# Attention scores: the low-half products of two maps on 64 rows each, side by side in the array

## The chip, the cores and the metric

The kernel runs on one core of a Trainium2 chip. The metric is the device time of one execution in microseconds (us). Engines are called as the profile calls them: PE (TensorE matmuls), PEld (TensorE weight loads), DVE (VectorE), ACT (ScalarE), POOL (GpSimd), SP (SyncE, which issues the DMAs).

## The reference

A two-layer encoder trunk in float32, sequence 1024, width 1024: a convolution and gating layer, an MLP, a differential attention layer, an MLP, each with a norm whose shift, scale and gate come from a condition vector. The part that matters is the attention, 8 heads of two softmax maps with 64 channels each:

```python
q = q.reshape(B, S, H, 2, d) * (d ** -0.5)      # d = 64, H = 8, S = 1024
k = k.reshape(B, S, H, 2, d)
v = v.reshape(B, S, H, 2 * d)
...
logits = (jnp.einsum('bqhjd,bkhjd->bhjqk', qb, k).astype(f32)
          + bias.astype(f32)[None, :, None])    # qb: 128 queries
p = jax.nn.softmax(logits, axis=-1)
attn = p[:, :, 0] - lam * p[:, :, 1]
return jnp.einsum('bhqk,bkhe->bqhe', attn.astype(v.dtype), v)
```

## The kernel before

PE takes its operands in a rounded type (`F32R`). For precision each operand is split into a high half (rounded) and a low half (the rest), and a product is made of three: high by high, high by low, low by high (`mm3`, lines 130 to 132). Everything is laid out with channels on partitions.

The attention runs head by head. `qkv(hd)` is a generator that projects the keys, queries and values of a head in six units (`UNITS`); it yields after every k-tile so that the products of the next head's projections can stand between those of this head's attention (`fill`, with counts from `QUOTA`). The last head has no next one, and the output projection's first part (`early`) fills in its place.

A map has 64 channels, half of the 128 rows of the array. The keys of map j are kept in one tile `K[j]` of 128 rows: for map 0 the high halves in rows 0 to 63 and the low halves in rows 64 to 127, for map 1 the other way round. The queries of a unit (512 queries) are kept in four tiles `Q`: high and low halves of map 0, high and low halves of map 1, each written to its own 64 rows by ACT (high) or DVE (low) and copied by a DMA to the other 64 rows. So one product of 128 rows by `Q[2j]` gives high by (high + low), and one by `Q[2j + 1]` gives low by (high + low).

`Head.softmax(qb)` makes the scores of 128 queries against 1024 keys for both maps. A map's scores `S` fill two banks of PSUM (`bufs=2`, so two maps' scores are alive at a time); each of its two halves of 512 keys is one product by the high queries (line 961) and one by the low ones (line 962). Then DVE adds the bias and takes the minimum (line 965), ACT the exponential (line 967), DVE combines both maps (line 975). `turn` transposes the result on PE (line 987) and splits it (ACT line 259, DVE line 260), and `values` multiplies it with the values for two query blocks at once (lines 998 to 1000).

The order on each engine is set by the framework's scheduler from the order in which the code is written, the dependencies, and priorities; engines then run their own lists in order and wait for each other on semaphores. There are 64 softmax blocks: 8 heads of 8 query blocks.

One product elsewhere is smaller than the array: the bias table (line 449), 32 rows and 8 columns, four products of two passes each, at 83 us.

Of the kernel before, what the change touches and what calls it, by code (L numbers as in the profile page):

```python
# [10 lines left out]
F32 = mybir.dt.float32  # L11
F32R = mybir.dt.float32r
AF = mybir.ActivationFunctionType
ALU = mybir.AluOpType
# [4 lines left out]
P = 128  # L19
D = 1024  # L20
T = 1024
KT = D // P
C = 512
NC = T // C
# [23 lines left out]
def trunk(ctx: ExitStack, tc: tile.TileContext, t_in, out):  # L48
    nc = tc.nc
    dve, act, pool, pe, sp = nc.vector, nc.scalar, nc.gpsimd, nc.tensor, nc.sync  # L50

    def f32(ap):
        return ap.bitcast(F32)
# [11 lines left out]
    NOSYNC = mybir.DependencyInfo(mybir.DependencyClass.NoSync, mybir.DependencyReason.DATA)  # L65
# [20 lines left out]
    def load(dst, src):  # L86
        sp.dma_start(out=dst, in_=src)
# [264 lines left out]
    with opened(name="mix", bufs=1) as mp, ExitStack() as pst:  # L352
# [87 lines left out]
        psum = pst.enter_context(opened(name="mixps", bufs=6, space=PSUM))  # L440
# [5 lines left out]
        for j in range(4):  # L446
            js = slice(j * C, (j + 1) * C)
            ps = bank()
# [10 lines left out]
        for j in range(2):  # L459
            dve.tensor_tensor_reduce(out=lv[:, 2 * j, :], in0=lv[:, 2 * j, :], in1=lv[:, 2 * j + 1, :], op0=ALU.mult,  # L460
                                     op1=ALU.add, scale=1.0, scalar=0.0, accum_out=ls[:, j:j + 1])
# [46 lines left out]
        for t in range(8):  # L508
            dve.tensor_scalar(out=vg[t], in0=vg[t], scalar1=mv[:, t, 0:1], scalar2=vr[:, t:t + 1],
                              op0=ALU.subtract, op1=ALU.mult)  # L510


        ps = bank()
        pe.matmul(ps, ones, sgw, start=True, stop=True)
        for g in range(4):
            dve.scalar_tensor_tensor(out=sgb[:, g, :], in0=ps[:, g * P:(g + 1) * P], scalar=vcol(V_SLB + g),
                                     in1=sgb[:, g, :], op0=ALU.mult, op1=ALU.add)
# [372 lines left out]
    if True:  # L890
# [6 lines left out]
        def qkv(hd):  # L897
            K = [ap.tile([P, T], F32R, name=f"K{j}", tag="K", bufs=4) for j in range(2)]
            Vh = ap.tile([P, KT, P], F32R, name="Vh", tag="V", bufs=4)
            Vl = ap.tile([P, KT, P], F32R, name="Vl", tag="V", bufs=4)  # L900
            Q = [None] * NC
            res = (K, Q, Vh, Vl)
            yield res
            for which, c in UNITS[hd > 0]:
                cs = slice(c * C, (c + 1) * C)
                wh, wl = ws.get(3 * hd + which)
                tick()
                ps = bank()
                for k in range(KT):
                    mm3(ps, wh[:, kcol(k)], wl[:, kcol(k)], h[k][c][0], h[k][c][1], k == 0, k == KT - 1)  # L910
                    if k < KT - 1:
                        yield None
                with tc.high_priority(offset=300):
                    if which == 0:
                        act.copy(out=K[0][0:64, cs], in_=ps[0:64])
                        act.copy(out=K[1][64:128, cs], in_=ps[64:128])
                        dve.tensor_tensor(out=K[0][64:128, cs], in0=ps[0:64], in1=f32(K[0][0:64, cs]), op=ALU.subtract)
                        dve.tensor_tensor(out=K[1][0:64, cs], in0=ps[64:128], in1=f32(K[1][64:128, cs]), op=ALU.subtract)
                    elif which == 1:
                        qs = [ap.tile([P, C], F32R, name="Q", tag="Q", bufs=10) for _ in range(4)]  # L920
                        Q[c] = qs
                        act.activation(out=qs[0][0:64], in_=ps[0:64], func=AF.Copy, scale=SC)
                        act.activation(out=qs[2][64:128], in_=ps[64:128], func=AF.Copy, scale=SC)
                        dve.scalar_tensor_tensor(out=qs[1][0:64], in0=ps[0:64], scalar=SC, in1=f32(qs[0][0:64]),
                                                 op0=ALU.mult, op1=ALU.subtract)
                        dve.scalar_tensor_tensor(out=qs[3][64:128], in0=ps[64:128], scalar=SC, in1=f32(qs[2][64:128]),
                                                 op0=ALU.mult, op1=ALU.subtract)
                        for q in (0, 1):
                            load(f32(qs[q][64:128]), f32(qs[q][0:64]))
                            load(f32(qs[2 + q][0:64]), f32(qs[2 + q][64:128]))  # L930
                    else:
                        vT = tmp.tile([P, C], F32, name="vT", tag="ss", bufs=2)
                        act.copy(out=vT, in_=ps)
                        pt = bank()
                        for n in range(4):
                            pe.transpose(pt[:, n * P:(n + 1) * P], vT[:, n * P:(n + 1) * P], ident)
                        vs = slice(c * 4, c * 4 + 4)
                        split(Vh[:, vs, :].rearrange("p a b -> p (a b)"), Vl[:, vs, :].rearrange("p a b -> p (a b)"), pt)
                yield None

        class Head:
# [9 lines left out]
            def softmax(self, qb, fill=None, between=0):  # L951
                c, qs = qb // 4, slice((qb % 4) * P, (qb % 4 + 1) * P)
                win = self.B[:, 896 - P * qb:896 - P * qb + T]
                E, s = [], small.tile([P, 2], F32, name="s", tag="s")
                for j in range(2):
                    if j and fill:
                        fill(between)
                    S = psum.tile([P, T], F32, name="S", tag="S", bufs=2)
                    for n in range(NC):
                        sl = slice(n * C, (n + 1) * C)  # L960
                        pe.matmul(S[:, sl], self.Q[c][2 * j][:, qs], self.K[j][:, sl], start=True, stop=False)
                        pe.matmul(S[:, sl], self.Q[c][2 * j + 1][:, qs], self.K[j][:, sl], start=False, stop=True)
                    L = apr.tile([P, T], F32, name="L", tag="E", bufs=4)
                    mn = small.tile([P, 1], F32, name="mn", tag="mn")
                    dve.tensor_tensor_reduce(out=L, in0=S, in1=win, op0=ALU.add, op1=ALU.min, scale=1.0,  # L965
                                             scalar=3e38, accum_out=mn)
                    act.activation(out=L, in_=L, func=AF.Exp, bias=mn, scale=-1.0, accum_out=s[:, j:j + 1])  # L967
                    E.append(L)

                if qb % 4 == 0:  # L970
                    self.se = small.tile([P, 4], F32, name="se", tag="se", bufs=3)
                r = small.tile([P, 1], F32, name="rs", tag="rs")
                dve.reciprocal(out=r, in_=s[:, 1:2])
                dve.scalar_tensor_tensor(out=r, in0=r, scalar=nlam, in1=s[:, 0:1], op0=ALU.mult, op1=ALU.mult)
                dve.scalar_tensor_tensor(out=E[0], in0=E[1], scalar=r, in1=E[0], op0=ALU.mult, op1=ALU.add)
                dve.scalar_tensor_tensor(out=self.se[:, qb % 4:qb % 4 + 1], in0=s[:, 0:1], scalar=SUB_EPS, in1=s[:, 0:1],
                                         op0=ALU.mult, op1=ALU.mult)
                if qb % 4 == 3:
                    load(sed[self.hd, c].rearrange("n p -> p n"), self.se)
                self.E = E[0]  # L980
# [236 lines left out]
```

## Time and profile before

| | |
|---|---|
| median of 3 runs | 2315.51 us (2313.82 to 2316.77) |
| the profiled execution | 2312.99 us, span 2311.2 us |
| PE busy | 2188.4 us (95%) |
| DVE busy | 1867.0 us (81%) |
| ACT busy | 1180.8 us (51%) |
| POOL busy | 238.5 us (10%) |
| granted TensorE clock, mean | 0.982 |
| scores, lines 961 and 962 | 256 + 256 products, first at 1035.5 us, last at 1583.5 us |

Busy times are those of one profiled execution. Matmuls overlap, and the profile models their ends: a matmul's duration is longer than its slot, the distance from its start to the next one's. PEld lists the loads of the stationary operand; a load that runs beside the matmul before it costs PE nothing.

### The profile page before, as it was taken

The page shows a single profiled execution, that of the slowest core. Times are in us where ns is not written, and L with a number is a line of the kernel's source. Part 1 is how long each engine was busy: PE and PEld are TensorE (multiplying, and loading weights), DVE is VectorE, ACT ScalarE, POOL GpSimd, SP SyncE. Part 2 cuts the span into 40 slices and gives each one's busy share as a digit, 9 for nine tenths or more (in the row PEclk, how much of TensorE's full clock was granted, in tenths as well). Part 3 has the DMA queues.
Part 4 walks back from the last instruction along what each step waited for, and adds up shares of the span by engine and source line. Part 5 has one row for each costly group of instructions (what it writes and reads, how often), then busy time and mean ns, then how long its engine had stood idle before and what let it go on. Part 6 is the DMA issues. An engine that isn't in the chain of part 4 may idle for free. (4 is left out here: it accounts for less than half of the span.)

```text
span 2311.2 us, 27508 instructions
## 1 busy us (share of the span) xinstructions
PE 2188.4 (95%) x10144; PEld 1800.3 (78%) x10144; DVE 1867.0 (81%) x2582; ACT 1180.8 (51%) x1753; POOL 238.5 (10%) x126
## 2 busy tenths in 40 slices
PE   4997599999999999979999999999999999999997
PEld 3786387778888888858888888887778888888886
DVE  8899899997785976986878878876699659578497
ACT  4554246643534535455666666654366354353455
POOL 0484000000000000031111111111100000000002
PEclk9998799999999999989999999999999999999999
DMA  8221553838448267233445333361353461643712
GB/s 319 84 73 46 192 168 131 319 112 284 178 165 284 97 224 250 91 114 90 93 92 109 68 90 73 77 205 51 114 216 121 163 229 48 214 140 111 245 45 73
DMA packets 113863, 335.17 MB, mean 145 GB/s; under 512 B 20576, under 2 KB 23520, under 8 KB 112704
## 3 DMA queue, kind: packets, MB, share of 16 engines
q1 hardware_dynamic: 113728, 333.41, 44.6%
q8 instruction: 80, 1.31, 0.2%
q14 instruction: 55, 0.45, 0.1%
HBM read 279.79 MB, written 53.58 MB: 144 GB/s over the span
## 5 line engine op out<-in xcount | busy, mean ns | idle before, releaser
L131 PE MATMUL ps<-b,whi 128*128 128x512 f32 (+1 forms) x1808 | 701.4, 389 | 6.7 <-DVE b L260 6.7
L130 PE MATMUL ps<-b,whi 128*128 128x512 f32 (+1 forms) x1808 | 692.8, 390 | 5.1 <-ACT b L259 4.6
L132 PE MATMUL ps<-b,wlo 128*128 128x512 f32 (+1 forms) x1808 | 693.6, 388 | 1.9 <-DVE wlo L260 1.9
L259 ACT CAST whi<-raw 128x1024 fp32r<-128x1024 f32 (+1 forms) x225 | 236.5, 1051 | 356.1 <-PE ps L131 310.1
L131 PEld LDWEIGHTS ps<-b,whi 128*128 128x128 f32 x1808 | 340.7, 188 | 79.7 <-DVE b L260 9.5
L130 PEld LDWEIGHTS ps<-b,whi 128*128 128x128 f32 x1808 | 340.3, 188 | 77.0 <-ACT b L259 3.9
L132 PEld LDWEIGHTS ps<-b,wlo 128*128 128x128 f32 x1808 | 340.4, 188 | 72.1 <-DVE wlo L260 2.7
L260 DVE TENSOR_TENSOR wlo<-raw,whi 128x1024 fp32r<-128x1024 f32 x224 | 273.0, 1219 | 137.4 <-ACT whi L259 135.5
L130 PE MATMUL ps<-hh,whi 128*128 128x512 f32 x576 | 225.0, 403 | 40.7 <-ACT hh L254 23.5
L131 PE MATMUL ps<-hl,whi 128*128 128x512 f32 x576 | 229.4, 399 | 4.1 <-DVE hl L255 2.6
L132 PE MATMUL ps<-hh,wlo 128*128 128x512 f32 x576 | 227.9, 396 | 0.0
L113 POOL TENSOR_TENSOR wlo<-raw,whi 128x1024 fp32r<-128x1024 f32 x32 | 83.7, 2619 | 1188.3 <-ACT whi L112 1027.4
L967 ACT ACTIVATE L<-L,mn 128x1024 f32<-128x1024 f32 x128 | 147.1, 1150 | 90.3 <-DVE mn L965 89.0
L748 DVE SCALAR_TENSOR_TENSOR x<-ps,mod,x 128x512 f32<-128x512 f32 x220 | 159.3, 744 | 38.6 <-PE ps L132 38.3
L965 DVE CUSTOM_DVE_ANT_0 L<-S,B 128x1024 f32<-128x1024 f32 x128 | 155.9, 1223 | 37.1 <-PE pt L987 18.2
L130 PEld LDWEIGHTS ps<-hh,whi 128*128 128x128 f32 x576 | 109.7, 191 | 67.9 <-ACT hh L254 27.2
L259 ACT CAST b<-f 128x512 fp32r<-128x512 f32 x192 | 118.0, 618 | 76.5 <-PE ps L132 74.6
L260 DVE TENSOR_TENSOR b<-f,b 128x512 fp32r<-128x512 f32 x192 | 128.6, 683 | 10.0 <-ACT b L259 10.0
L131 PEld LDWEIGHTS ps<-hl,whi 128*128 128x128 f32 x576 | 110.5, 192 | 29.3 <-DVE hl L255 5.5
L132 PEld LDWEIGHTS ps<-hh,wlo 128*128 128x128 f32 x576 | 110.4, 192 | 24.1 <-issue 0.5
L147 DVE CUSTOM_DVE_ANT_0 mraw<-mraw,cact 128x1024 f32<-128x1024 f32 x96 | 116.1, 1217 | 6.2 <-DMA mraw<-in_modw 6.2
L737 ACT COPY f<-ps 128x512 f32<-128x512 f32 x96 | 56.3, 590 | 122.8 <-PE ps L132 122.6
(199 smaller groups left out, 3478.8 us busy)
## 6 DMA issues: line engine op xcount, KB each, us to landing
b<-tspl SPq DMA_DIRECT2D x168, 512.0 KB, 5.2
raw<-in_wm SPq DMA_DIRECT2D x128, 512.0 KB, 4.3
mraw<-in_modw SPq DMA_DIRECT2D x96, 512.0 KB, 4.6
tspl<-b SPq DMA_DIRECT2D x56, 512.0 KB, 4.2
raw<-in_wqkv SPq DMA_DIRECT2D x24, 512.0 KB, 4.7
raw<-in_wo SPq DMA_DIRECT2D x17, 512.0 KB, 3.5
x<-in_xT SPq DMA_DIRECT2D x32, 256.0 KB, 5.8
tsr<-tsp SPq DMA_DIRECT2D x8, 1024.0 KB, 7.7
```

Source lines behind the costliest of these rows:

```text
L113: (eng or dve).tensor_tensor(out=lo, in0=raw, in1=f32(hi), op=ALU.subtract)
L130: pe.matmul(ps, wh, ah, start=first, stop=False, skip_group_check=resumed)
L131: pe.matmul(ps, wh, al, start=False, stop=False, skip_group_check=resumed)
L132: newest[0] = pe.matmul(ps, wl, ah, start=False, stop=last, skip_group_check=resumed)
L147: i = dve.tensor_tensor_reduce(out=raw, in0=raw, in1=cact, op0=ALU.mult, op1=ALU.add, scale=1.0, scalar=0.0, accum_out=acc)
L259: act.copy(out=out_h, in_=src)
L260: (lo_eng or dve).tensor_tensor(out=out_l, in0=src, in1=f32(out_h), op=ALU.subtract)
L737: act.copy(out={"X1": c11, "Y1": c22, "X2": c12}[p], in_=ps)
L748: dve.scalar_tensor_tensor(out=x[m][c], in0=ps, scalar=gate(d, m), in1=x[m][c], op0=ALU.mult, op1=ALU.add)
L965: dve.tensor_tensor_reduce(out=L, in0=S, in1=win, op0=ALU.add, op1=ALU.min, scale=1.0, scalar=3e38, accum_out=mn)
L967: act.activation(out=L, in_=L, func=AF.Exp, bias=mn, scale=-1.0, accum_out=s[:, j:j + 1])
```

## The change

The queries of a unit get three tiles instead of four: the high halves of map 0 and map 1 as before (written to their own 64 rows, copied by DMA to the others), and one tile for the low halves of both maps, map 0 in rows 0 to 63 and map 1 in rows 64 to 127, without a copy. The scores of both maps are allocated before either is reduced. The products by the high halves stay as they are, all 128 rows. The products by the low halves now use only the 64 rows of their own map, in which `K[j]` holds the high keys; the product of low queries with low keys is left out. In the built program these products are laid on the upper half of the array's rows for map 0 and on the lower half for map 1, all 128 columns; for each half of the keys map 0's and map 1's stand one after the other, and an ordering dependency without a semaphore keeps the four behind the last product by the high halves and in their order.

```diff
-                        qs = [ap.tile([P, C], F32R, name="Q", tag="Q", bufs=10) for _ in range(4)]
+                        qs = [ap.tile([P, C], F32R, name="Q", tag="Q", bufs=9) for _ in range(3)]
                         Q[c] = qs
                         act.activation(out=qs[0][0:64], in_=ps[0:64], func=AF.Copy, scale=SC)
-                        act.activation(out=qs[2][64:128], in_=ps[64:128], func=AF.Copy, scale=SC)
-                        dve.scalar_tensor_tensor(out=qs[1][0:64], in0=ps[0:64], scalar=SC, in1=f32(qs[0][0:64]),
-                                                 op0=ALU.mult, op1=ALU.subtract)
-                        dve.scalar_tensor_tensor(out=qs[3][64:128], in0=ps[64:128], scalar=SC, in1=f32(qs[2][64:128]),
-                                                 op0=ALU.mult, op1=ALU.subtract)
-                        for q in (0, 1):
-                            load(f32(qs[q][64:128]), f32(qs[q][0:64]))
-                            load(f32(qs[2 + q][0:64]), f32(qs[2 + q][64:128]))
+                        act.activation(out=qs[1][64:128], in_=ps[64:128], func=AF.Copy, scale=SC)
+                        for j in range(2):
+                            own, other = slice(64 * j, 64 * j + 64), slice(64 - 64 * j, 128 - 64 * j)
+                            dve.scalar_tensor_tensor(out=qs[2][own], in0=ps[own], scalar=SC, in1=f32(qs[j][own]),
+                                                     op0=ALU.mult, op1=ALU.subtract)
+                            load(f32(qs[j][other]), f32(qs[j][own]))
...
+                S = []
                 for j in range(2):
                     if j and fill:
                         fill(between)
-                    S = psum.tile([P, T], F32, name="S", tag="S", bufs=2)
+                    S.append(psum.tile([P, T], F32, name="S", tag="S", bufs=2))
                     for n in range(NC):
                         sl = slice(n * C, (n + 1) * C)
-                        pe.matmul(S[:, sl], self.Q[c][2 * j][:, qs], self.K[j][:, sl], start=True, stop=False)
-                        pe.matmul(S[:, sl], self.Q[c][2 * j + 1][:, qs], self.K[j][:, sl], start=False, stop=True)
+                        before = pe.matmul(S[j][:, sl], self.Q[c][j][:, qs], self.K[j][:, sl], start=True, stop=False)
+                for n in range(NC):
+                    sl = slice(n * C, (n + 1) * C)
+                    for j in range(2):
+                        rows = slice(64 * j, 64 * j + 64)
+                        i = pe.matmul(S[j][:, sl], self.Q[c][2][rows, qs], self.K[j][rows, sl], start=False, stop=True)
+                        tc.add_manual_dep(i.ins, before.ins.name, NOSYNC, reason="side by side")
+                        before = i
+                for j in range(2):
                     L = apr.tile([P, T], F32, name="L", tag="E", bufs=4)
                     mn = small.tile([P, 1], F32, name="mn", tag="mn")
-                    dve.tensor_tensor_reduce(out=L, in0=S, in1=win, op0=ALU.add, op1=ALU.min, scale=1.0,
+                    dve.tensor_tensor_reduce(out=L, in0=S[j], in1=win, op0=ALU.add, op1=ALU.min, scale=1.0,
```

In the lists below `S_` are the scores, `K0` and `K1` the keys of the two maps, `Q_` the query tiles, `pt_` the transposes, `AT_` their split; numbers tell buffers apart. Line numbers of the changed kernel are 4 to 7 higher from the scores on: its line 966 makes the products of 64 rows, 994 the transposes, 1005 and 1006 the products with the values.

PE, the first softmax of a query half in the second head. Before:

```order
L961 MATMUL S_8695<-K0_7812,Q_8284 128x512 [waits DMAHW3_49,DVE_49]
L962 MATMUL S_8695<-K0_7812,Q_8285 128x512 [waits DMAHW6_49]
L961 MATMUL S_8695<-K0_7812,Q_8284 128x512
L962 MATMUL S_8695<-K0_7812,Q_8285 128x512
L961 MATMUL S_8710<-K1_7813,Q_8286 128x512 [waits DMAHW4_49,DVE_49]
L962 MATMUL S_8710<-K1_7813,Q_8287 128x512 [waits DMAHW7_49]
L987 MATMUL pt_8567<-ident_75,L_8441 128x128 [waits DVE_49,PE_49]
L987 MATMUL pt_8567<-ident_75,L_8441 128x128 x7
L961 MATMUL S_8710<-K1_7813,Q_8286 128x512
L962 MATMUL S_8710<-K1_7813,Q_8287 128x512
```

Now:

```order
L961 MATMUL S_8683<-K0_7806,Q_8275 128x512 [waits DMAHW2_49,DVE_49]
L961 MATMUL S_8683<-K0_7806,Q_8275 128x512
L961 MATMUL S_8692<-K1_7807,Q_8276 128x512 [waits DMAHW3_49,DVE_49]
L961 MATMUL S_8692<-K1_7807,Q_8276 128x512
L966 MATMUL S_8683<-K0_7806,Q_8277 128x512
L966 MATMUL S_8692<-K1_7807,Q_8277 128x512
L966 MATMUL S_8683<-K0_7806,Q_8277 128x512
L966 MATMUL S_8692<-K1_7807,Q_8277 128x512
```

The four products by the low halves, which stood behind a product by the high half each, stand together at the end of the block, the two maps in turn; nothing stands between them.

PE, two softmax blocks later in the same head, from the transposes to the first products with the values. Before:

```order
L987 MATMUL pt_8737<-ident_75,L_8587 128x128 x7
L961 MATMUL S_8915<-K0_7812,Q_8284 128x512 [waits DVE_49]
L962 MATMUL S_8915<-K0_7812,Q_8285 128x512
L961 MATMUL S_8915<-K0_7812,Q_8284 128x512
L962 MATMUL S_8915<-K0_7812,Q_8285 128x512
L998 MATMUL ps_8809<-AT_8681,Vh_7814 128x256 [waits Activation_49]
L936 MATMUL ps_8883<-ident_75,vT_8881 128x128 x4
L961 MATMUL S_8930<-K1_7813,Q_8286 128x512 [waits DVE_49]
L962 MATMUL S_8930<-K1_7813,Q_8287 128x512
L961 MATMUL S_8930<-K1_7813,Q_8286 128x512
L962 MATMUL S_8930<-K1_7813,Q_8287 128x512
L999 MATMUL ps_8809<-AT_8682,Vh_7814 128x256 [waits DVE_49]
```

Now:

```order
L994 MATMUL pt_8725<-ident_75,L_8586 128x128 x7
L961 MATMUL S_8749<-K0_7806,Q_8275 128x512 [waits DVE_49]
L961 MATMUL S_8749<-K0_7806,Q_8275 128x512
L131 MATMUL ps_8758<-hl_7401,whi_8612 128x512
L961 MATMUL S_8765<-K1_7807,Q_8276 128x512 [waits DVE_49]
L961 MATMUL S_8765<-K1_7807,Q_8276 128x512
L966 MATMUL S_8749<-K0_7806,Q_8277 128x512
L966 MATMUL S_8765<-K1_7807,Q_8277 128x512
L966 MATMUL S_8749<-K0_7806,Q_8277 128x512
L966 MATMUL S_8765<-K1_7807,Q_8277 128x512
L132 MATMUL ps_8758<-hh_7400,wlo_8613 128x512
L1005 MATMUL ps_8794<-AT_8669,Vh_7808 128x256 [waits Activation_49]
```

Where the first product with the values stood behind four score products and the next behind four more, now a whole block of both maps stands between the transposes and the first of them.

## The prediction

> **What bounds the kernel now.** I read the page first (busy time per engine, granted clock), then the groups by line for the score products, then a table by stretch over the attention stage, then the waits of PE in it, and last the order of time around the one place where this kernel already leaves the full array. First the stage, 1052 to 1583 us, then one whole head:
>
> ```profile
> span 2311.2 us, 27508 instructions
> ...
> 1052.00:1583.00 531.00, 527.08 (x2877) 447.21 (x2876) 431.41 (x708) 323.66 (x508) 82.27 (x39) 1.00 0.42 96
> ...
> 1143.30:1212.50 69.20, 69.02 (x381) 58.78 (x380) 56.23 (x92) 42.73 (x68) 10.72 (x5) 1.00 0.46 91
> ...
> L961 PE MATMUL S<-K,Q 128*128 128x512 f32 x256 | 108.4, 424 | 0.6 <-DVE mn L965 0.6
> ...
> L962 PE MATMUL S<-K,Q 128*128 128x512 f32 x256 | 100.8, 394 | 0.0
> ```
>
> The columns of the table are the stretch, its length, and busy time of PE, PEld, DVE, ACT and POOL, then the granted clock. PE is busy in 527 of 531 us at clock 1.00; DVE, the next, in 56.2 of a head's 69.2 us. So each slot taken from PE here shortens the run, down to DVE's 56 us per head, which is 13 us away. The score products are 512 matmuls in 64 softmax blocks (8 heads, 8 query blocks), 8 in each; half of them (L962) use the low halves.
>
> The mean of 394 or 424 ns is no cost: matmuls overlap. What one costs is the distance between starts:
>
> ```profile
> 1322.86 0.39 PE L132 MATMUL ps<-hh,wlo 128*128 128x512 f32 x1
> ...
> 1325.13 0.39 PE L961 MATMUL S<-K,Q 128*128 128x512 f32 x1
> 1325.35 0.39 PE L962 MATMUL S<-K,Q 128*128 128x512 f32 x1
> ...
> 1324.90 0.19 PEld L961 LDWEIGHTS S<-K,Q 128*128 128x128 f32 x1
> 1325.13 0.19 PEld L962 LDWEIGHTS S<-K,Q 128*128 128x128 f32 x1
> ```
>
> Ten slots from 1322.86 to 1325.13 make 0.227 us each, and each load starts when the matmul ahead of it starts (1325.13 in both lists), so loads are hidden. A softmax block costs 8 x 0.227 = 1.82 us, 116 us in all.
>
> **The change: what it removes.** Four full products by the low halves become four of 64 rows, in two pairs. If a pair took one slot and nothing else changed, a block would lose 2 x 0.227 = 0.454 us, 64 blocks 29.1 us. That is the ceiling, 2283.9 us against the profiled execution's 2312.99.
>
> **What it adds: two changes of the array's shape per block.** All products here use 128 rows, so the trace of before shows no 64-row product. It has one place with a smaller shape, 32 rows and 8 columns (L449, the bias table). Starts around it, PE first, then PEld:
>
> ```profile
> 82.99 0.39 PE L132 MATMUL ps<-hh,wlo 128*128 128x512 f32 x1
> 83.31 1.02 PE L449 MATMUL ps<-oh,tb 32*8 32x512 f32 x2
> ...
> 85.89 1.02 PE L449 MATMUL ps<-oh,tb 32*8 32x512 f32 x2
> 86.84 0.50 PE L130 MATMUL ps<-hh,whi 128*128 128x512 f32 x1
> 87.18 0.39 PE L131 MATMUL ps<-hl,whi 128*128 128x512 f32 x1
> ...
> 82.77 0.19 PEld L132 LDWEIGHTS ps<-hh,wlo 128*128 128x128 f32 x1
> 83.31 0.09 PEld L449 LDWEIGHTS ps<-oh,tb 32*8 32x8 f32 x2 [0.35 <-issue]
> 83.75 0.08 PEld L449 LDWEIGHTS ps<-oh,tb 32*8 32x8 f32 x1 [0.34 <-issue]
> ...
> 86.84 0.19 PEld L130 LDWEIGHTS ps<-hh,whi 128*128 128x128 f32 x1 [0.86 <-issue]
> 86.94 0.19 PEld L131 LDWEIGHTS ps<-hl,whi 128*128 128x128 f32 x1
> ```
>
> Into the small shape: the last full matmul starts at 82.99, its slot ends at 83.22, and the next load starts only at 83.31, though in a full stream it would have started at 82.99. So the load is no longer hidden, and 0.09 us pass first. Out of it: the L449 slots are 0.43 us ((85.89 - 83.31) / 6), the last ends at 85.89 + 2 x 0.43 = 86.75, and the load of L130 starts 0.09 us later, at 86.84, "issue" being time in which it waited for nothing that the profile shows. L131 starts at 87.18, so L130 streamed from 86.95: its exposed load cost 0.11 us. Is the cause the other type (32-bit passes) rather than the shape? At full shape a change of type shows no gap:
>
> ```profile
> 1315.85 0.40 PE L132 MATMUL ps<-hh,wlo 128*128 128x512 f32 x1
> 1316.08 1.02 PE L1011 MATMUL ps<-sq,ones_r 128*128 128x512 f32 x2
> ...
> 1317.17 0.39 PE L962 MATMUL S<-K,Q 128*128 128x512 f32 x1
> ...
> 1315.85 0.42 PEld L1011 LDWEIGHTS ps<-sq,ones_r 128*128 128x128 f32 x2
> ```
>
> From 1316.08 to 1317.17 lie one score slot (0.227) and two 32-bit passes, 0.43 each; the first load was hidden at 1315.85. So the 0.43 of L449 is the type, and the gaps are the shape. I take 0.09 + 0.11 at each change of shape. The bounds are 0 (a change to 64 rows with all columns kept may be milder than to 32 x 8) and this price.
>
> Now a block, in us from the start of its last full product (slot ends 0.227). Load of the first half at 0.32; it streams from 0.43. The next load starts at 0.43, by the 0.10 us between the loads at 86.84 and 86.94, so the second half streams from 0.54. The first half's second product waits for its rows until 0.43 + 0.227 = 0.66, its partner's load starts then and it streams from 0.77 to 1.00. Drain 0.09, exposed load 0.11: the next full product streams at 1.20. Before, it came at 5 x 0.227 = 1.135. The block is 0.06 us **longer**: 64 x 0.062 = **+4.0 us**. Bounds: -0.454 per block (all hidden, -29.1 us) and +0.403 (same prices, halves one after the other: 0.43 + 4 x 0.227 + 0.20 = 1.54, +25.8 us).
>
> A load needn't wait for its own rows to finish: the load at 83.75 starts while the products of the same 32 rows run, one each 0.43 us from 83.31 on. [...]
>
> **Order around it.** The section on the change shows PE's rows of one block. The four small products stand together, so a block changes shape twice, not eight times; map 0 is finished only after map 1's full products, and DVE's reductions of both maps start together, where one used to follow each map.
>
> **What waits move.** PE's waits in the stage are small:
>
> ```profile
> PE ps L998 <- ACT AT L259: 1.6, 7, 0.5
> PE ps L999 <- DVE AT L260: 1.3, 2, 0.7
> PE S L961 <- DVE mn L965: 0.6, 2, 0.4
> ...
> L965 DVE CUSTOM_DVE_ANT_0 L<-S,B 128x1024 f32<-128x1024 f32 x125 | 152.2, 1223 | 33.8 <-PE pt L987 17.5 <-PE S L962 11.8
> ...
> L260 DVE TENSOR_TENSOR AT<-pt,AT 128x1024 fp32r<-128x1024 f32 x60 | 73.3, 1221 | 9.7 <-ACT AT L259 9.7
> ...
> L259 ACT CAST AT<-pt 128x1024 fp32r<-128x1024 f32 x60 | 60.6, 1010 | 5.5 <-PE pt L987 5.1
> ```
>
> A score buffer is free after its reduction (1.22 us). In the new order PE has at least 3.8 us of slots between the end of a block and the next write to map 0's buffer, and 4.1 for map 1's, counted from the order with 0.227 per 512-wide, 0.12 per 256-wide slot and 0.1 per transpose; DVE needs 1.2 and 2.4 plus at most about one 1.2 us split ahead of them. That fits: nothing. If the cover goes, it costs up to the missing 1.2 us in a block.
>
> The products with the values wait for the split of the transposes. In the second place that the section on the change shows, the first of them stood four score slots (0.9 us) behind the transposes and met ACT's 1.01 us cast; the second (L999) waits for DVE's split. In the new order the whole block stands between. About 2.3 us lie there now (six slots of 0.227 and the four small products, 1.20 - 0.23 with their drains), so the cast (1.01) is over; the second values product needs DVE's split too, 1.01 + 1.22 + gaps = 2.5 us, and may wait 0.1 to 0.2. I take **-1.0 us** of the 2.9 us of such waits (bounds -2.9, all gone, and +1.5, 0.2 us more at 8 places).
>
> **DMA and vector work.** Two of the four copies of Q per unit go (64 become 32 of 128 KB); DVE's two subtractions per unit stay, only their tile differs.
>
> ```profile
> Q<-Q SPq DMA_DIRECT2D x64, 128.0 KB, 4.2
> ```
>
> PE's wait rows show none on Q's copies, so I put this at 0; what covers it is that copies run a head ahead. No queue gets more work.
>
> **Sum** against the profiled execution: 2312.99 + 4.0 - 1.0 = 2316.0. That execution lies 2.5 us below the median of the runs, 2315.51; on the median the forecast is **2318.5 us**. What a measurement can tell from no change is 0.2%, 4.6 us.
>
> **Rivals.**
> (1) No drain between 128 and 64 rows, loads hidden. For it: the only rows with a drain are of a 32 x 8 shape, so row tiles with all columns may be spared. Against it: the gap stands at both ends there. It gives -29.1 - 1.0 with both halves starting together, -22.0 - 1.0 with the 0.11 us step between their starts (the next full product at 0.79): 2285 to 2293. A drain on one side only leaves about -10.
> (2) The loads of the two halves run side by side, as they use different rows. Then the second half starts with the first and each block is 0.11 us shorter than in my sum: -3.3 - 1.0, 2311.2. Against it: two loads of the full array stand 0.10 us apart; for it no row speaks. [...]
> (3) The other side, slower: the halves don't overlap at all, each taking a slot (the array or its way into PSUM serves one stream of these 4-byte operands at a time). Nothing in the trace shows two products side by side, for or against. A block is then 0.403 us longer: +25.8 - 1.0, 2340.3. It decides early: 0.03 us more in a block than in my sum is slower by over 0.2%. That the change doesn't do what it says is this case too.
> (4) A load waits until the running product of its own rows is over: the first half's second product loads at 0.66 and streams from 0.77, its partner from 0.88 to 1.10, the next full product at 1.30: +10.8 - 1.0, 2325.3. The row of 83.75 speaks against it. Near it lies another: DVE's two reductions, now back to back, hold PE at the score buffers; 0.2 us in each block would add 13.
>
> **How the numbers follow.** Forecast 0.35 (its own range 2313 to 2324: 0.25 of it within 0.2%, 0.08 slower, 0.02 faster); (1) 0.22, nearly all faster; (2) 0.15, faster in 0.06; (3) 0.18, slower; (4) 0.10, slower in 0.06. Faster 0.29, same 0.39, slower 0.32. The range runs from the milder part of (1) to (3): 2295 to 2341 leaves out the full gain of (1) without a drain (0.12) and anything worse than (3) (0.08).
>
> **What would show it.** In the changed profile: 512 score matmuls still, 256 with 64 rows; the first 64-row load about 0.32 us behind the last full start and the first full load 0.09 us behind the last half's slot (drains); the starts within a pair about 0.11 us apart and pairs 0.23 apart (if 0.23 between all four, rival 3; if both are 0 and loads hidden, rival 1). PE's busy share stays, DVE's reductions come in twos, and PE's waits on the scores stay under 2 us. I am wrong if the change of shape costs nothing, or if the halves go one by one.

## The result and the profile after

The change made the kernel slower: 2328.05 us (median of 4 runs, 2326.34 to 2333.26) against 2314.98 for the kernel before (4 runs on the same chip), a ratio of 1.0064, 95% interval 1.0051 to 1.0077, or 13.1 us. The profiled execution took 2326.36 us, its span is 2324.6 us, 13.4 longer than before.

First the table by stretch, with the columns that the prediction explains (the last two are the DMA engines' share and GB/s): the attention stage, one inner head, and the last head, which has the output projection beside it.

```profile
1052.00:1583.00 531.00, 518.00 (x2844) 410.32 (x2843) 416.82 (x697) 319.88 (x499) 75.15 (x37) 1.00 0.45 88
1143.30:1212.50 69.20, 68.69 (x381) 54.65 (x380) 55.05 (x92) 42.77 (x68) 10.05 (x6) 1.00 0.47 83
1519.70:1593.90 74.20, 66.01 (x348) 51.24 (x347) 52.81 (x89) 37.11 (x57) 11.36 (x6) 0.95 0.45 122
```

The inner head is nearly as full as before (68.69 of 69.20 us, before 69.02). In the last stretch PE stands idle for 8 us (before 2.8) and the granted clock is 0.95 (before 1.00). Now PE's waits from the start of attention into the stage that follows (total, times, longest):

```profile
PE ps L130 <- DMA th<-osp: 7.4, 2, 3.9
PE ps L130 <- DVE v L1022: 3.5, 1, 3.5
PE ps L1005 <- ACT AT L259: 2.2, 2, 1.1
PE pt L994 <- DVE AT L260: 2.0, 6, 0.3
PE ps L935 <- ACT vT L932: 1.8, 2, 1.1
...
PE ps L130 <- PE S L966: 1.0, 6, 0.2
PE ps L1006 <- DVE AT L260: 0.5, 1, 0.5
```

Before the change the largest in the same stretch were those on the values:

```profile
PE ps L998 <- ACT AT L259: 3.8, 9, 1.1
...
PE ps L999 <- DVE AT L260: 1.3, 2, 0.7
```

No wait on the scores is left, and those on the values shrank from 5.1 to 2.7 us, but the first two rows are new. The order of time says where they are (in brackets the idle time and its releaser):

```profile
1548.19 0.62 PE L130 MATMUL ps<-th,whi 128*128 128x512 f32 x1 [3.93 <-DMA th<-osp]
...
1582.13 0.88 PE L130 MATMUL ps<-th,whi 128*128 128x512 f32 x2 [3.45 <-DMA th<-osp]
...
1634.28 0.80 PE L130 MATMUL ps<-th,whi 128*128 128x512 f32 x1 [3.53 <-DVE v L1022]
```

Wait 1 and wait 2 are in the last head: PE waits for head 6's normed output (`th`, `tl`), which goes to DRAM (`osp`) and is fetched back for the output projection, once for each half of the queries. Wait 3 is behind attention: the first product of the next stage writes the PSUM bank in which the last norm's statistics (line 1018) still wait for DVE. These three are 10.9 us; around and behind them the granted clock is lower (0.95 from 1525 to 1560 us, 0.96 from 1560 to 1600 and from 1600 to 1640; before, 1.00 in all three).

### One block

The block itself did not get longer. Its rows, PE first, then PEld:

```profile
1328.49 0.40 PE L961 MATMUL S<-K,Q 128*128 128x512 f32 x1
1328.82 0.49 PE L966 MATMUL S<-K,Q 64*128 64x512 f32 x1
...
1329.15 0.40 PE L966 MATMUL S<-K,Q 64*128 64x512 f32 x2
1329.48 0.49 PE L132 MATMUL ps<-hh,wlo 128*128 128x512 f32 x1
...
1328.81 0.19 PEld L966 LDWEIGHTS S<-K,Q 64*128 64x128 f32 x2 [0.37 <-issue]
...
1328.92 0.19 PEld L966 LDWEIGHTS S<-K,Q 64*128 64x128 f32 x2
...
1329.48 0.19 PEld L132 LDWEIGHTS ps<-hh,wlo 128*128 128x128 f32 x1 [0.36 <-issue]
```

Both first loads start together, 0.32 us behind the last full start. Both second loads start at 1328.92, while the first pair streams through the same rows, so they are hidden. Over the 63 blocks with this pattern the medians from the last full start are: first pair 319 and 322 ns, second pair 656 and 659, next full start 983, the one after it 1318. That next full product streams from 1318 - 227 = 1.09 us, where it was 1.135 before: 0.045 us **shorter**, 2.9 us over 64 blocks.

### Where the output of head 6 gets late

The last reductions of head 1 and head 6, after and then before:

```profile
1182.56 1.22 DVE L972 CUSTOM_DVE_ANT_0 L<-S,B 128x1024 f32<-128x1024 f32 x1
...
1528.97 1.22 DVE L972 CUSTOM_DVE_ANT_0 L<-S,B 128x1024 f32<-128x1024 f32 x1
```

```profile
1172.37 1.23 DVE L965 CUSTOM_DVE_ANT_0 L<-S,B 128x1024 f32<-128x1024 f32 x1 [0.46 <-PE pt L987]
...
1518.49 1.22 DVE L965 CUSTOM_DVE_ANT_0 L<-S,B 128x1024 f32<-128x1024 f32 x1 [0.47 <-PE pt L987]
```

A head takes 69.28 us ((1528.97 - 1182.56) / 5), before 69.22: no loss from head to head, and no gain either. But every softmax stands 10 us later against the rest. The wait for both maps is not enough to explain this: the score products themselves stand later in PE's built list. The first of head 1 starts at 1119.50 instead of 1108.91 us, and the last block of head 6 at 1524.77 instead of 1511.7; between the first score product of all and that block stand 1056 projection products (lines 130 to 132) instead of 1032. Why the scheduler put them there was not followed. The rest of PE's stream is not late: its first product with `th` starts at 1539.45, before at 1539.68.

What the 10 us move is one small DMA. The store of the softmax sums (`sed<-se`) writes 512 single 4-byte elements (from 1568 to 1572 us, where nothing else moves, the trace has 528 packets, all under 512 B) and waits for the last reduction. SP's issues in the last head, after and then before:

```profile
1531.94 0.51 SPq L87 DMA_DIRECT2D sed<-se  x1
...
1536.21 0.33 SPq L87 DMA_DIRECT2D osp<-oh  x1
1536.85 6.14 SPq L87 DMA_DIRECT2D raw<-in_wo  x2
1543.10 0.38 SPq L87 DMA_DIRECT2D osp<-ol  x1
1545.43 0.33 SPq L87 DMA_DIRECT2D th<-osp  x1
...
1569.26 0.37 SPq L87 DMA_DIRECT2D sed<-se  x1
1571.75 0.32 SPq L87 DMA_DIRECT2D osp<-oh  x1
1573.26 0.32 SPq L87 DMA_DIRECT2D osp<-ol  x1
1579.16 0.32 SPq L87 DMA_DIRECT2D th<-osp  x1
```

```profile
1520.00 0.37 SPq L87 DMA_DIRECT2D sed<-se  x1
...
1536.18 0.33 SPq L87 DMA_DIRECT2D osp<-oh  x1
...
1538.56 0.33 SPq L87 DMA_DIRECT2D osp<-ol  x1
1539.98 0.33 SPq L87 DMA_DIRECT2D th<-osp  x1
...
1554.52 0.37 SPq L87 DMA_DIRECT2D sed<-se  x1
1566.48 0.32 SPq L87 DMA_DIRECT2D osp<-oh  x1
1568.62 0.32 SPq L87 DMA_DIRECT2D osp<-ol  x1
1569.03 0.38 SPq L87 DMA_DIRECT2D th<-osp  x1
```

Before, the store was issued 12 to 16 us ahead of head 6's output; now 2.5 to 4.3 us ahead. From the issue of `osp<-oh` to its fetch were 2.6 to 3.8 us, now 7.4 to 9.2. In the first case SP itself stands still: the two issues of `raw<-in_wo` take 6.14 us, since one waits 5.5 us for "DMA sed<-se", and `osp<-ol` is queued behind them. The DMA engines' busy tenths from 1572 to 1580 us after the change, in slices of 0.2 us, show the second case:

```profile
DMA  0019993000599908010000009000000000000000
```

The data of `osp<-oh` and `osp<-ol` have moved by 1575.2, and but for two slices the engines are idle from then on; SP, whose wait there is "DMA osp<-oh", goes on only at 1579.16, 9.9 us after the issue of `sed<-se`. The small store's packets had moved by 1570.5, but it is reported landed only 8.7 us behind its issue, at 1577.91, and SP's wait for the bulk store ends 1.25 us behind that. So here the bulk store isn't told as landed before the small one is. That the one waits for the other is my reading: these rows show no single engine's writes, and the trace has no landing time for this bulk store.

### The profile page after: what moved, and what is told of

Its sections match the earlier page's. It is cut to its first block, busy times and chain, and to the rows that moved or that the text cites. A ratio compares the mean times of both kernels' runs of the same rounds, so it can differ in the third digit from the quotient of the medians.

```text
span 2324.6 us, 27390 instructions
## 1 busy us (share of the span) xinstructions
PE 2189.5 (94%) x10144; PEld 1769.6 (76%) x10144; DVE 1859.2 (80%) x2582; ACT 1182.6 (51%) x1753; POOL 233.5 (10%) x126
## 4 chain that ended last, share of the span: by engine, by line
PE 78%; DVE 13%; DMA 2%; issue 2%; POOL 2%; ACT 2%; SPq 0%; DVEq 0%; ACTq 0%; POOLq 0%
PE ps L130 22%; PE ps L131 22%; PE ps L132 22%; PE pt L994 2%; PE S L961 2%; POOL a L596 2%; DVE ca L600 2%; PE S L966 2%; PE ps L1006 1%; PE ps L1005 1%; PE ps L1007 1%; DVE ht L242 1%; DVE ss L233 1%; DVE mraw L147 1%; DVE wlo L113 1%
## 5 line engine op out<-in xcount | busy, mean ns | idle before, releaser
L113 POOL TENSOR_TENSOR wlo<-raw,whi 128x1024 fp32r<-128x1024 f32 x32 | 77.8, 2431 | 1160.2 <-ACT whi L112 1120.8
L972 DVE CUSTOM_DVE_ANT_0 L<-S,B 128x1024 f32<-128x1024 f32 x128 | 151.2, 1218 | 18.2 <-PE S L966 18.2
```

Of the source, the lines that this page charges most:

```text
L113: (eng or dve).tensor_tensor(out=lo, in0=raw, in1=f32(hi), op=ALU.subtract)
L972: dve.tensor_tensor_reduce(out=L, in0=S[j], in1=win, op0=ALU.add, op1=ALU.min, scale=1.0, scalar=3e38, accum_out=mn)
```

## The experiments

### The array's shape

The first kernel keeps the changed order and takes the shape away:

```diff
-  i = pe.matmul(S[j][:, sl], self.Q[c][2][rows, qs], self.K[j][rows, sl], start=False, stop=True)
+  i = pe.matmul(S[j][:, sl], self.Q[c][2][:, qs], self.K[j][:, sl], start=False, stop=True)
```

> The changed kernel with one thing undone: the four small products of a block multiply all 128 rows (tile Q[2] against all of K[j]) instead of 64, so that the array keeps its shape and nothing streams side by side. The order of every engine is that of the changed kernel. (The low products then take in rows of the other map: only the time is meant.) Theory A (the trace of the changed kernel: a block is 1.09 us instead of 1.135, so the shape brings 64 x 0.045 = 2.9 us, and the loss of 13.1 us lies in the order, in three waits of the last head and the tail): 2328 to 2331 us, as slow as the changed kernel or up to 2.9 us slower, with the same three waits of PE (about 4.1 and 3.6 us in front of the products of head 6, 3.5 us in front of the pool that follows). Theory B (the array's shape is the cost, 13.1 / 64 = 0.2 us in a block): 2315 us, as before the change.

Measured: 2329.76 us (6 runs), ratio 1.0061 (1.0046 to 1.0076). Its trace has the same waits ("DMA th<-osp" 7.6 us, "DVE v L1022" 3.4). Theory A: the loss is there without any 64-row product, so it is the order's.

The second has the order of before and changes the shape twice for each map:

```diff
-  pe.matmul(S[:, sl], self.Q[c][2 * j][:, qs], self.K[j][:, sl], start=True, stop=False)
-  pe.matmul(S[:, sl], self.Q[c][2 * j + 1][:, qs], self.K[j][:, sl], start=False, stop=True)
+  before = pe.matmul(S[:, sl], self.Q[c][2 * j][:, qs], self.K[j][:, sl], start=True, stop=False)
+for n in range(NC):
+  i = pe.matmul(S[:, sl], self.Q[c][2 * j + 1][rows, qs], self.K[j][rows, sl], start=False, stop=True)
```

> The kernel before, in its own order, but each map's two low products use the 64 rows that hold that map's low halves, one after the other, so that a block changes the array's shape four times instead of twice and no two products lie side by side (the low halves' products with the low half of K are left out). Price of the shape by the changed kernel's trace: from the start of the last full product to the next full one that streams 0.425 + 0.227 + 0.227 + 0.10 + 0.11 = 1.09 us for two small products, against 3 x 0.227 = 0.68 before: +0.41 us in each of 128 maps, +52 us, 2367 us. If a load also had to wait for the running product of its own rows, 0.11 us more in each map: 2381 us. If the shape of the array costs nothing and the gaps of the changed kernel come from something else in its blocks: 2315 us.

Measured: 2365.58 us (4 runs), ratio 1.0221 (1.0208 to 1.0234): +51.5 us against the expected 52. The price of the shape is there without the changed order, and there is no sign of a wait for a load's own rows. That the sum came out so well is in part luck. In the built order something stands between the two small products in 19 of the 128 maps, so the shape changes to 64 rows and back 147 times, not 128, and by time each costs 0.35 us. The trace has the 0.41 us in the 109 unbroken maps (medians: the next full product's record 987 ns behind the last full one's, streaming 0.10 us later), and PE's waits on values and scores are 2.8 us instead of 5.7, which hides a part.

The third issues the four small products twice:

```diff
-  for n in range(NC):
+  for r, n in ((0, 0), (0, 1), (1, 0), (1, 1)):
...
-    ..., start=False, stop=True)
+    ..., start=False, stop=r == 1)
```

> The changed kernel with the four small products of a block issued twice (the low part is added twice). Two more pairs in each of 64 blocks. If the two products of a pair stream together in one slot of 0.227 us and the loads of the next pair are hidden: 2 x 0.227 x 64 = +29 us on 2328, 2357 us. If the loads wait for the running product of the same rows (0.11 us more in a pair): +43, 2371 us. If the two products take a slot each: 4 x 0.227 x 64 = +58, 2386 us.

Measured: 2368.02 us (4 runs), 40 us above the changed kernel, between the first two forecasts. In its trace the pairs of unbroken blocks start 319, 654, 888 and 1122 ns behind the last full product (38 blocks, medians), so a hidden pair costs 0.234 us and the block grows by 0.468, 30 us in all. But in the built order 26 of the 64 blocks stand in two groups, with the transposes or others between, and change shape twice more: 26 x 0.41 = 10.7 us. The sum is 40.6. Two products do share one slot.

### The queue and the bank

Four kernels took away one or the other cause that the trace names, and won little.

```diff
+ dve.memset(bank()[:, 0:1], 0.0)         # first thing in the stage behind attention
```

> The changed kernel with one tiny write added at the start of the stage after attention, which takes the first buffer of the new pool in PSUM, so that the stage's first product goes to the next bank and no longer to the one that holds the last head's statistics. Theory A: the wait of 3.5 us in front of that product (on DVE's step of the last norm) goes, and with it up to 1 us of reduced clock behind it: 2323.5 to 2325 us. Rival: PE only meets the next late thing behind it (the normed tiles of the last head, which DVE and ACT finish just as late), and nothing is won: 2327 to 2328 us.

Measured: 2328.22 us (5 runs), ratio 1.0061 (1.0049 to 1.0073), nothing won. The wait on "DVE v" is gone from its trace, where "DMA th<-osp" is 8.3 us. The expected 4 us are hardly more than the comparison resolves, so what this wait is worth alone stays open.

```diff
+ dve.memset(bank()[:, 0:1], 0.0)
- load(raw[:, m, :], t_in["wo1"][m][:, kcol(KT - 1)])
+ i = sp.dma_start(out=raw[:, m, :], in_=t_in["wo1"][m][:, kcol(KT - 1)])
+ tc.add_manual_dep(i.ins, mark[0].ins.name, NOSYNC, reason="not before")   # a product of tile m = 1
```

> The changed kernel with the tiny write that moves the next pool's first product to another PSUM bank, and with the four 64 KB loads of raw weights (raw<-in_wo, 128x128) issued behind the stores and fetches of head 6's output instead of between them, so that SP no longer waits there for the 4-byte store of the softmax sums. Theory A (the loss is the three waits of the last head): the waits before head 6's first tile (4.1 us) and at the next pool (3.8) go, the second tile's (3.6) stays: 2328 - 7.9 = 2320 us, and 2318.5 if the reduced clock behind the first wait goes too. Rival: the time won at the first tile is lost at the second, whose stores come when DVE's norm is done: the wait there grows from 3.6 towards 7 and the kernel is at 2323 to 2325 us. If the waits are not the loss: 2328.

Measured: 2325.91 us (5 runs), ratio 1.0049 (1.0036 to 1.0062), nearer to the rival. PE's order of time in it:

```profile
1549.61 0.50 PE L130 MATMUL ps<-th,whi 128*128 128x512 f32 x1 [1.53 <-DMA th<-osp]
...
1584.60 1.22 PE L130 MATMUL ps<-th,whi 128*128 128x512 f32 x2 [3.83 <-DMA th<-osp]
```

SP now issues both stores at once, 1.4 us apart, and still waits 7.2 us for `osp<-oh`: SP's order was a part of wait 1, the landing is the rest.

```diff
- load(sed[self.hd, c].rearrange("n p -> p n"), self.se)
+ act.dma_start(out=sed[self.hd, c].rearrange("n p -> p n"), in_=self.se)
+ dve.memset(bank()[:, 0:1], 0.0)
```

> The changed kernel with the same tiny write, and with the store of the softmax sums (sed<-se, single 4-byte elements, about 10 us to landing) issued on ACT's queue instead of SP's. PE's order and the places of the raw weights stay as in the changed kernel. Theory A (that store stands ahead of head 6's output in SP's queue, and holds up what follows): both waits of PE on head 6's tiles go (4.1 and 3.6 us), and the one at the next pool (3.8): 2316.5 us, 2315 with the reduced clock behind them gone. Rival B (head 6's output is late because DVE's norm comes 5 us later, whatever the queue): the second wait stays, 2320 us. Rival C (ACT is held up while it issues the stores, 16 times): each would show as a wait on ACT's casts of up to 1 us, up to 16 us more than by A.

Measured: 2327.52 us (5 runs), ratio 1.0054 (1.0042 to 1.0066). Theory A failed in its word "queue". ACT issues the store at 1574.28 on a queue of its own, and SP's stores land as late as before:

```profile
1574.28 0.37 ACTq L986 DMA_DIRECT2D sed<-se  x1
```

```profile
1576.75 0.32 SPq L87 DMA_DIRECT2D osp<-oh  x1
...
1584.54 0.32 SPq L87 DMA_DIRECT2D th<-osp  x1
```

From store to fetch are 7.79 us, with the small store on SP's queue 7.41: on another queue it did not free what follows it here. The control has the same two edits on the kernel before:

> A control: the kernel before with the same two edits (the tiny write, and the store of the softmax sums on ACT's queue). Its trace has none of the three waits, so both edits have nothing to take away: 2314 to 2316 us. If they bring time of their own, 16 stores off SP's queue for instance, it is below 2312, and what v_act wins is then not the change's loss alone.

Measured: 2315.52 us (12 runs), ratio 1.0003 (0.9989 to 1.0017): they bring nothing there.

The fourth has other numbers of projection tiles in the last head:

```diff
-QUOTA_LAST = [(2, 2, 0, 0), (2, 2, 1, 1)] * 3 + [(0, 2, 0, 0), (0, 4, 0, 0)]
+QUOTA_LAST = [(1, 1, 0, 0), (1, 1, 1, 0)] + [(2, 2, 0, 0), (2, 2, 1, 1)] * 2 + [(2, 2, 0, 0), (2, 4, 0, 0)]
```

> The changed kernel with other numbers of projection tiles at each block of the last head: fewer at the first two blocks (1, 1 and 1, 1, 1 instead of 2, 2 and 2, 2, 1, 1), more at the last two, so that head 6's tiles are needed some 5 tiles (5 x 0.69 = 3.4 us) later; queues as in the changed kernel. Theory A: the first wait (4.1 us) shrinks to under 1 us and the second (3.6) too, the one at the next pool stays: 2320 to 2322 us. Rival: the blocks with fewer tiles no longer cover ACT's cast and DVE's splits (1.01 and 1.22 us), and PE waits there for what it saves: 2326 to 2330 us.

Measured: 2327.55 us (5 runs), ratio 1.0056 (1.0044 to 1.0068). The time lies in the rival's range, but not by its mechanism: PE's waits for casts and splits of the values are 2.3 us, against 2.7 in the changed kernel. The two waits on `th`, which theory A had at under 1 us each, total 9.7. The later need was no help; why they grew was not followed further.

### The store's place in time

The deciding edit leaves all queues as they are and issues two of the sixteen small stores behind head 6's output instead of ahead of it:

```diff
-  load(sed[self.hd, c].rearrange("n p -> p n"), self.se)
+  if (self.hd, c) in ((H - 2, 1), (H - 1, 0)):
+      held.append((self.hd, c, self.se))
+  else:
+      load(sed[self.hd, c].rearrange("n p -> p n"), self.se)
...
-  tick(9)
-  fetch(k, c)
+  behind = fetch(k, c)                    # now returns the fetch of tl
+  for hd_, c_, se in held:
+      i = sp.dma_start(out=sed[hd_, c_].rearrange("n p -> p n"), in_=se)
+      tc.add_manual_dep(i.ins, behind.ins.name, NOSYNC, reason="behind")
+  held.clear()
+  tick(9)
```

> The changed kernel with one thing moved: two of the sixteen stores of softmax sums (sed<-se, 512 single 4-byte elements; those of head 6's second half and head 7's first) are issued on SP behind the store and fetch of head 6's output (osp, th, tl) instead of ahead of them. Their readers come 10 us or more later. Theory A (what keeps head 6's output from landing is that store's own transfer on the DMA engines, whichever queue issues it): osp<-oh lands in 3 to 4 us as before the change instead of 5.5 to 7, both waits of PE on th<-osp (4.1 and 3.6 us) go, the one at the next pool (3.8) stays: 2320.5 us, 2319 with the reduced clock behind the waits gone. Rival B (the burst of fetches ahead of it, and DVE's later norm, hold it up): the waits stay at more than half, 2324 to 2328 us.

Measured: 2324.44 us (6 runs), ratio 1.0050 (1.0034 to 1.0067). SP's issues around the second half:

```profile
1573.60 0.32 SPq L87 DMA_DIRECT2D osp<-oh  x1
1575.11 0.32 SPq L87 DMA_DIRECT2D osp<-ol  x1
1575.65 0.32 SPq L87 DMA_DIRECT2D th<-osp  x1
...
1577.59 0.39 SPq L1071 DMA_DIRECT2D sed<-se  x1
```

From store to fetch 2.05 us instead of 7.4, and no wait on `th` is left in the trace:

```profile
PE ps L1008 <- ACT AT L259: 4.1, 3, 1.9
PE ps L130 <- DVE v L1025: 3.4, 1, 3.4
```

The mechanism is theory A's; the time won, 3.6 us, is half of what A said, and by time alone not clear of noise (this interval overlaps that of the changed kernel, 1.0051 to 1.0077). A part was given back at the next cover: PE reaches the values products sooner and waits 1.9 us more for ACT's cast and 0.6 more for DVE's split. Wait 3 stays, as expected. The same edit with the other two:

> The same two stores held back, and with it the tiny write that moves the next pool's first product to another PSUM bank, and the four 64 KB raw weights behind the stores of head 6's output. Theory A: all three waits of the last head are gone, and what is left of the change is a block 0.045 us shorter, less 0.04 us a head lost to DVE's splits: 2315 to 2317 us, level with the kernel before; the reductions stay 10 us later than before the change all the same. Rival: something else is late next, 2319 to 2322 us.

Measured: 2316.49 us (11 runs), ratio to the kernel before 1.0009 (1.0000 to 1.0017). Theory A: 11.6 of the 13.1 us are back, without a change to the products. The reductions still stand 11 us later than before the change (the last of head 6 at 1529.58 us), so their lateness by itself is not the loss. Of the three waits none is left, and the granted clock from 1525 to 1560 us is 1.00 instead of 0.95; the kernel before, the changed one and this one:

```profile
1525.00:1560.00 35.00, 34.02 (x188) 28.47 (x187) 28.71 (x47) 19.94 (x32) 6.88 (x3) 1.00 0.54 165
1525.00:1560.00 35.00, 30.73 (x164) 23.49 (x163) 24.05 (x39) 17.17 (x27) 5.54 (x3) 0.95 0.69 186
1525.00:1560.00 35.00, 34.57 (x195) 27.00 (x193) 27.14 (x46) 20.75 (x34) 6.14 (x3) 1.00 0.53 166
```

Two reservations: in the first half the fetch still comes 6.1 us behind `osp<-oh` (1534.75 to 1540.88), with no small store in SP's list between 1515 us and this fetch. Eight fetches of 256 KB were issued just ahead, from 1529.06 us on, and may be what delays it; that isn't shown, but wait 1 need not be the small store's alone. And holding the stores back and loading the raw weights later were not tried on the kernel before, whose trace has none of the three waits.

The other way round, one store delayed in the kernel before, in its own order:

```diff
+  for hd_, c_, se in held:                # head 6's second half, behind the first fetches of early()
+      i = sp.dma_start(out=sed[hd_, c_].rearrange("n p -> p n"), in_=se)
+      tc.add_manual_dep(i.ins, behind.ins.name, NOSYNC, reason="behind")
```

> The kernel before, with its own order and products, and one store of softmax sums (head 6's second half) issued 12 us later, behind the last burst of fetches and just ahead of the stores of head 6's output, where the changed kernel has it. Theory A (the store's place is the loss): a wait of PE on th<-osp of 2 to 4 us comes up in front of head 6's first tile, 2317.5 to 2320 us. Rival B (it is the later work on DVE): no wait, 2315 us.

Measured: 2322.21 us (5 runs), ratio 1.0032 (1.0020 to 1.0044), 7.5 us slower than the kernel before, by one DMA of 2 KB. Its waits and its stretch from 1525 to 1560 us:

```profile
PE ps L130 <- DMA th<-osp: 4.9, 1, 4.9
```

```profile
1525.00:1560.00 35.00, 30.10 (x154) 25.36 (x153) 23.48 (x38) 16.57 (x25) 7.02 (x3) 0.90 0.61 128
```

The loss is above the forecast: the wait is 4.9 us where 2 to 4 were expected, and the clock granted there fell to 0.90 (kernel before: 1.00), to which I put down the rest.

Last, what the shape is worth once nothing waits: the version without the three waits, with the small products on all rows.

> The version with the three waits taken away (stores of softmax sums held back, bank moved, raw weights later), and in it the four small products of a block on all 128 rows as in the first experiment (so the low products take in rows of the other map; only the time is meant). Same order on every engine. Theory A (the shape's 0.045 us a block, 0.065 by the first experiment's own block, reaches the end once nothing else waits): 64 x 0.045 to 0.065 = 2.9 to 4.2 us slower than 2316.5, 2319.4 to 2320.7 us. Theory B (DVE's splits set the pace of a head, and take back what the shape gives, as the head's period of 69.43 instead of 69.28 us in the first experiment says): 7 x 0.15 = 1 us slower, 2317.5 us.

Measured: 2315.91 us (12 runs), ratio 1.0009 (1.0000 to 1.0018), the same as with 64 rows. Theory B fits, theory A's 2.9 us and more do not show. The traces put a size to B: an inner head takes 69.46 us with the small products on all rows and 69.28 with 64, so the shape brings 0.18 us a head, of the 0.43 by which its eight blocks are shorter (1.09 instead of 1.145 us each in this order); over seven heads that is 1.2 us, less than these runs can tell apart. No version was found that beats the kernel before.

## Why the prediction was right in part, by its steps

The 2328.05 us lie in the range (2295 to 2341), and "slower" had 0.32. That it lies inside is luck: the upper part of the range stood there for rival 3, two halves that don't overlap, and that rival is out. The forecast was 2318.5, and the sum of its steps, +3.0 us, met the measured +13.1 with another composition.

- **Slot and ceiling** (0.227 us, -29.1): the slot stands. Pairs share it.
- **Two changes of shape in a block** (0.09 drain, 0.11 exposed load, read off the 32 x 8 bias table): right. The first 64-row load comes at 0.32 us as foretold, and the second experiment shows 0.41 us for the two changes around a map's pair.
- **The step of 0.10 to 0.11 us within a pair**: wrong, and this is the term of the products that was mis-sized. I read it off two loads of the full array; the halves' loads and starts stand 3 ns apart. The block is -0.045 us instead of +0.062, -2.9 us instead of +4.0. That is rival 2, which had 0.15. Rivals 1, 3 and 4 are out: there is a drain (0.09 us from the last full slot to the first 64-row load), the halves overlap (0.234 us a pair in the third experiment), and the loads at 1328.92 start while their own rows stream (from 1328.82).
- **Values' waits** (-1.0): those on ACT and DVE went from 2.9 to 0.5 us in the stage, more than foretold. But transposes now wait 2.0 us on DVE's split and 1.0 us goes at the first product behind a block, once each in six heads, which with the block's -0.36 us a head leaves the period about unchanged.
- **"Each slot taken from PE here shortens the run"**: too strong. In the first experiment, which has the order without the shape, an inner head takes 69.45 us: the order costs 0.22 us a head against the kernel before, and of the 0.5 us by which its eight blocks are longer than the changed kernel's only 0.16 reach the period.
- **Score buffers**: right, no wait.
- **DMA and vector work, 0**: this is the step that failed. "No queue gets more work" was true and beside the point. I had written that map 0 is finished only after map 1's products and DVE's reductions start together, but followed it only to PE's buffers, not to what DVE's results release on SP. The scores and reductions come 10 us later in the built order, a store of 2 KB moves to just ahead of the last head's output, and PE waits 7.4 us for it; wait 3, the bank, came with the new order as well. The runs put 11.6 us on the three waits together, clock included.

From the trace: -2.9 (blocks) - 2.4 (values) - 0.6 (scores) + 3.0 (transposes and behind blocks) + 1.6 (`vT`, 1.8 us where it was 0.2) + 10.9 (the three waits) = +9.6 us. The rest of the 13.1 I put down to the reduced clock behind the three waits; it was not divided further.

## What to carry to other kernels

Where an edit delays a result without lengthening anything, follow the result to every DMA that waits for it, and look at what that DMA then stands ahead of; a queue's work can be unchanged and its order in time costly. Keep scattered stores of a few bytes well away from bulk transfers that somebody waits for: here 7.41 us passed from store to fetch with such a store 2.5 us ahead and 2.05 without, and another queue did not separate them (7.79). Read a gain at the head's period, not at the block: here the blocks are 0.43 us a head shorter than with full products in the same order, and 0.18 us arrived.

## What was not expected of the hardware

- Two products of 64 rows in different halves start 3 ns apart and share a slot of 0.227 to 0.234 us, loads included; a load of rows in use starts 0.10 us into the product on them (1328.92) and is hidden. But a block changes shape twice, at some 0.2 us each (0.09 to 0.10 until the next load, 0.11 for that load), so its four small products save only 0.045 to 0.063 us against four full ones.
- With a store of 512 single 4-byte elements, 2 KB, issued 2.5 us ahead of a 256 KB store, the fetch that waits for the latter was issued 7.41 us behind it (7.79 with the small store on ACT's queue), against 2.05 us with the small store issued later.
- Waits of PE came with a lower clock: from 1525 to 1560 us it was 0.95 around a wait of 3.9 us and 0.90 around one of 4.9 us, against 1.00 in the kernel before and in the version without the three waits. It was 0.95 around the 1.53 us of the second edit of queue and bank too, and 0.96 from 1560 to 1600 us in the version without the three waits, so the length of the wait alone does not give it. One added wait of 4.9 us went with a loss of 7.5 us.
